# First norm of a decoder trunk in four quarters of the features, seven column tiles of the first FFN fed by each

## The chip, the core and the metric

The kernel runs on one core of one Trainium2 chip. The metric is device time in microseconds (us) of one execution. The core has five engines with a queue each, worked off in order: TensorE (PE, its weight loads PEld), VectorE (DVE), ScalarE (ACT), GpSimd (POOL) and SyncE (SP), which here only issues DMAs. Engines wait for each other and for DMAs by semaphores.

## The reference

Two layers act on a residual stream h of 512 tokens by 1024 features. Each sub-layer first normalises h, then scales and shifts it by numbers that come from a condition vector c:

```python
cond = jax.nn.silu(c)
for l in range(DEPTH):
    mod = cond @ ada_w[l] + ada_b[l]                      # 9 x 1024 numbers
    sh1, sc1, g1, sh2, sc2, g2, sh3, sc3, g3 = jnp.split(mod, N_MOD, axis=-1)
    hn = _modulate(_rms_norm(h, norm_g[l, 0]), sh1, sc1)  # xn * (1 + scale) + shift
    h = h + 0.5 * g1[:, None, :] * _swiglu(hn, ffn1_w_in[l], ffn1_w_out[l])
    hn = _modulate(_rms_norm(h, norm_g[l, 1]), sh2, sc2)
    z = hn @ w_in[l]
    ...                                                   # four token mixers, then w_out
    hn = _modulate(_rms_norm(h, norm_g[l, 2]), sh3, sc3)
    h = h + 0.5 * g3[:, None, :] * _swiglu(hn, ffn2_w_in[l], ffn2_w_out[l])

def _swiglu(x, w_in, w_out):
    gate, up = jnp.split(x @ w_in, 2, axis=-1)
    return (jax.nn.silu(gate) * up) @ w_out
```

The FFN is 2816 wide. What matters here is the very first norm: nothing of the first FFN can start before `sh1`, `sc1` (a product of c with 8 MB of weights) and the root mean square of x are there.

## The kernel before, in words

**Layout.** h is kept with features on the partitions: 8 tiles `h[k]` of 128 features x 512 tokens. Every product of the FFN is made three times, since each fp32 number is split into a high and a low fp32r part: `mm3` (L300 to 307) does high x high (L303), low activation x high weight (L304), high activation x low weight (L305). Weights come in chunks of [128, 2048]: a DMA on SP into a `raw` buffer (three of them), then `split_piece` rounds a part of it on ScalarE to `wh` (L271) and subtracts on VectorE to `wl` (L272). `proj_fm` opens four PSUM banks (pool `mm`) and runs them through the 8 feature tiles in two chunks of 4. A second PSUM pool, `at`, has four banks for everything small.

**The FFN.** `ffn` goes through the 22 hidden tiles in three parts (6, 8, 8). For each pair of hidden tiles one `proj_fm` makes two gate and two up tiles; the tile `i`. When a part's hidden tiles are done, the products with `w_out` follow; the tile `o`. Before the first `o` product stand 6 hidden tiles x 2 (gate, up) x 8 feature tiles x 3 = 288 products of 128x512.

**The start.** x comes in two DMAs (L386). ScalarE squares it (L598), TensorE transposes it into PSUM, ScalarE copies it to `h[k]` (L603). `rsqrt` (L177 on) takes the reciprocal root on VectorE, `bcast_tokens` spreads it over the partitions by TensorE (`bc_n`), and it stays in PSUM. `first_load` brings the weights of `sc1` (j = 1) and `sh1` (j = 0) by halves of the features (512 columns, rows of 2 KB). `partial_sums` adds up weight x cond over 8 tiles k: on VectorE (`accV`, L626 and 628) or as a product on ScalarE (L630, 633) that GpSimd adds (`accA`, L634); `SHARE` says which k goes where. `first_mod` sums over the partitions on TensorE (`adaps`), and VectorE adds the bias (`modc`, L646, 649). `scaled` makes `hn` on VectorE (L655), `shifted` rounds it to `hnh` on ScalarE (L659) and takes the rest `hnl` on VectorE (L660). `warm` is a run of products whose result nobody reads.

The first half of the features is done before the first FFN product; the second is done by `second_half`, which is issued between the first products. Later modulation weights come in steps of 1 MB (`ada_load`, `ada_step`: L454, 456), four to a group of 1024 numbers, with a reduction on VectorE (L465, 466) and one product by `fold` (also named `adaps`).

**What sets the order.** The code is recorded in a loop with a virtual clock for the helpers; then a scheduler orders the instructions of each engine and places buffers. `issue_after` only says what an instruction must stand behind on its own engine.

Of the kernel before, what the change touches and what calls it, by code (L numbers as in the profile page):

```python
# [24 lines left out]
def tile_hybrid_trunk(  # L25
# [49 lines left out]
    S1, S2, RS0, W0, W1 = 2.0, 3.0, 0, 20, 30  # L75
    SHARE = {(1, 0): "VVVVVVVV", (0, 0): "AAVVAAVV", (1, 1): "AAVVAVVV", (0, 1): "AVVVAVVV"}
# [184 lines left out]
    def split_piece(n, q):
# [50 lines left out]
    def proj_fm(name, nchunks, act, ks, evac, ranges=(FULL,), before=None):  # L312

        ps = [mmt(f"{name}_{m}") for m in range(4)]
        got = []
        for ri, (a, b) in enumerate(ranges):
# [3 lines left out]
            for ci in range(nchunks):  # L320
                if ci == 1 and not ahead[0]:
                    finish(startup)
                    ahead[0] = 2
# [4 lines left out]
                for m in range(4):  # L328
# [99 lines left out]
    def ada_load(n, tag="raw"):  # L428
# [76 lines left out]
    def first_load(j, e, tag):  # L505
        for q in range(2):
            r = wpool.tile([P, 2048], F32, tag=tag[q], name=f"fw{j}{e}{q}").rearrange("p (k d) -> p k d", k=4)
            src = ada_w[0, 4 * q * P : (4 * q + 4) * P, j * D + e * 512 : j * D + (e + 1) * 512]
            nc.sync.dma_start(out=r, in_=src.rearrange("(k p) d -> p k d", p=P))
            first_w[j, e, q] = r  # L510

    first_load(1, 0, ("raw", "raw"))
    first_load(0, 0, ("raw", "wl"))
    load_chunk(0)
    first_load(1, 1, ("wh", "wh"))
    first_load(0, 1, ("raw", "raw"))
# [97 lines left out]
    def partial_sums(j, e, q):  # L614


        for k in range(4 * q, 4 * q + 4):
            src = first_w[j, e, q][:, k % 4, :]
            how = SHARE[j, e][k]
            new = (j, e, how) not in begun  # L620
            if new:
                begun[j, e, how] = blk(name=f"acc{how}")
            acc = begun[j, e, how]
# [657 lines left out]
```

## Time and profile before

| | |
|---|---|
| median of 3 runs | 2001.35 us (2001.15 to 2002.89) |
| profiled execution | 1998.79 us |
| its span, first to last instruction | 1997.0 us |
| TensorE busy | 1960.0 us, 98% of the span |
| VectorE, ScalarE, GpSimd busy | 62%, 36%, 1% |
| DMA | 250.56 MB, mean 125 GB/s |
| mean granted clock of TensorE | 0.992 |

The table is of one execution, whose time stands 2.56 us below the median. A busy TensorE is not TensorE at its peak, since matmuls overlap: the pace is read from start to start. A granted clock of 1.00 is 2.4 GHz, 0.50 is 1.2 GHz.

### The profile page before, as it was taken

What the parts mean: (1) busy time and instruction counts of PE and PEld (TensorE: products, weight loads), DVE (VectorE), ACT (ScalarE), POOL (GpSimd) and SP (SyncE); (2) the same over time, 40 slices, a digit from 0 to 9 for tenths busy, and PEclk for the clock granted to TensorE, in tenths of its full rate; (3) what the DMA queues carried; (4) which work ended last, traced back from release to release, by engine and by line L of the source; (5) the groups of instructions that cost most, each with busy time, mean ns of one, the idle gap of its engine ahead of it and who ended that gap; (6) DMA issues with size and microseconds to landing.
All of it is one profiled execution on the core that took longest, in us unless ns stands there. A gap on an engine that the chain in (4) does not pass through costs nothing.

```text
span 1997.0 us, 26246 instructions
## 1 busy us (share of the span) xinstructions
PE 1960.0 (98%) x10339; PEld 1673.0 (84%) x10339; DVE 1230.1 (62%) x2595; ACT 726.4 (36%) x1513; POOL 24.3 (1%) x48
## 2 busy tenths in 40 slices
PE   7999999999999999999999999999999999999999
PEld 6788888897889888888898888889887898888888
DVE  7776765488877777676675433337898683333332
ACT  4323222344774423222342232333376543232230
POOL 2000000000000000000000000000000000000000
PEclk9999999999999999999999999999999999999999
DMA  8666655232211466566434323232212122423321
GB/s 286 215 203 208 214 189 186 85 91 64 69 43 47 154 201 231 184 217 211 148 106 147 118 93 106 85 106 91 64 64 70 43 64 85 127 86 104 106 64 43
DMA packets 157640, 250.56 MB, mean 125 GB/s; under 512 B 5748, under 2 KB 100428, under 8 KB 157516
## 3 DMA queue, kind: packets, MB, share of 16 engines
q1 hardware_dynamic: 156928, 247.73, 37.7%
q8 instruction: 81, 1.33, 0.3%
q0 software_dynamic: 352, 1.05, 0.2%
q14 instruction: 43, 0.35, 0.1%
q10 hardware_dynamic: 236, 0.10, 0.0%
HBM read 246.76 MB, written 2.10 MB: 125 GB/s over the span
## 4 chain that ended last, share of the span: by engine, by line
PE 93%; DVE 4%; ACT 1%; issue 1%; POOL 0%; DMA 0%; SPq 0%; ACTq 0%; POOLq 0%
PE i L304 16%; PE i L305 16%; PE i L303 16%; PE o L303 8%; PE o L304 8%; PE o L305 8%; PE wo L303 1%; PE wo L305 1%; PE wo L304 1%; PE scA L144 1%; PE scD L144 1%; PE poA L144 1%; DVE wl L272 1%; PE poD L144 1%; DVE cacc L953 1%
## 5 line engine op out<-in xcount | busy, mean ns | idle before, releaser
L272 DVE TENSOR_TENSOR wl<-w,wh 128x512 fp32r<-128x512 f32 (+2 forms) x664 | 410.6, 666 | 320.0 <-ACT wh L271 319.4
L271 ACT CAST wh<-w 128x512 fp32r<-128x512 f32 (+2 forms) x664 | 360.3, 602 | 655.8 <-issue 370.1
L304 PE MATMUL i<-hnl,wh 128*128 128x512 f32 (+1 forms) x1504 | 566.9, 378 | 4.0 <-DVE hnl L660 3.7
L303 PE MATMUL i<-hnh,wh 128*128 128x512 f32 (+1 forms) x1504 | 565.0, 378 | 4.1 <-ACT hnh L568 2.2
L305 PE MATMUL i<-hnh,wl 128*128 128x512 f32 (+1 forms) x1504 | 565.6, 377 | 0.0
L304 PEld LDWEIGHTS i<-hnl,wh 128*128 128x128 f32 x1504 | 284.2, 189 | 57.3 <-DVE hnl L660 6.0
L303 PEld LDWEIGHTS i<-hnh,wh 128*128 128x128 f32 x1504 | 283.2, 189 | 55.8 <-ACT hnh L568 2.6
L305 PEld LDWEIGHTS i<-hnh,wl 128*128 128x128 f32 x1504 | 284.3, 189 | 51.5
L303 PE MATMUL o<-acth,wh 128*128 128x512 f32 (+1 forms) x832 | 297.8, 358 | 0.0
L304 PE MATMUL o<-actl,wh 128*128 128x512 f32 (+1 forms) x832 | 296.7, 357 | 0.0
L305 PE MATMUL o<-acth,wl 128*128 128x512 f32 (+1 forms) x832 | 296.6, 356 | 0.0
L305 PEld LDWEIGHTS o<-acth,wl 128*128 128x128 f32 x832 | 157.2, 189 | 22.7
L303 PEld LDWEIGHTS o<-acth,wh 128*128 128x128 f32 x832 | 157.2, 189 | 22.4
L304 PEld LDWEIGHTS o<-actl,wh 128*128 128x128 f32 x832 | 157.2, 189 | 22.3
L456 DVE SCALAR_TENSOR_TENSOR acc<-ada,cond,acc 128x512 f32<-128x512 f32 x224 | 154.8, 747 | 32.1 <-DMA ada<-in_ada_w_dram 31.9
L776 DVE TENSOR_TENSOR silu<-silu,i 128x512 f32<-128x512 f32 x88 | 60.4, 687 | 170.5 <-PE i L305 170.5
L778 ACT CAST acth<-silu 128x512 fp32r<-128x512 f32 x88 | 54.4, 618 | 238.5 <-DVE silu L776 238.3
L708 DVE SCALAR_TENSOR_TENSOR h<-o,modc,h 128x512 f32<-128x512 f32 (+1 forms) x112 | 74.0, 671 | 70.8 <-PE o L305 70.2
L953 DVE SCALAR_TENSOR_TENSOR cacc<-yp,cwc,cacc 128x512 f32<-128x512 f32 x120 | 89.5, 746 | 1.6
L780 DVE TENSOR_TENSOR actl<-silu,acth 128x512 fp32r<-128x512 f32 x88 | 60.6, 689 | 28.2 <-ACT acth L778 28.2
L775 ACT ACTIVATE silu<-i 128x512 f32<-128x512 f32 x88 | 52.4, 595 | 37.1 <-PE i L305 37.1
L568 ACT ACTIVATE hnh<-hn,modc 128x256 fp32r<-128x256 f32 x80 | 38.8, 506 | 72.2 <-DVE hn L567 72.2
(298 smaller groups left out, 2228.4 us busy)
## 6 DMA issues: line engine op xcount, KB each, us to landing
w<-in_ffn_w_in_dram SPq DMA_DIRECT2D x176, 512.0 KB
ada<-in_ada_w_dram SPq DMA_DIRECT2D x64, 1024.0 KB
w<-in_ffn_w_out_dram SPq DMA_DIRECT2D x40, 1024.0 KB
w<-in_w_in_dram SPq DMA_DIRECT2D x18, 1024.0 KB
fw<-in_ada_w_dram SPq DMA_DIRECT2D x8, 1024.0 KB
w<-in_w_out_dram SPq DMA_DIRECT2D x8, 1024.0 KB
w<-in_ffn_w_out_dram SPq DMA_DIRECT2D x8, 512.0 KB
w<-in_w_in_dram SPq DMA_DIRECT2D x4, 520.0 KB
```

The costliest lines, as they stand in the source:

```text
L144: return T.matmul(out, **kw)
L271: A.copy(wh[:, a], r[:, a])
L272: V.tensor_tensor(wl[:, a], r[:, a], wh[:, a].bitcast(F32), ALU.subtract)
L303: T.matmul(ps, lhsT=lh, rhs=rh, start=start, stop=False)
L304: T.matmul(ps, lhsT=lh, rhs=rl, start=False, stop=False)
L305: last_t[0] = T.matmul(ps, lhsT=ll, rhs=rh, start=False, stop=stop)
L456: last_v[0] = V.scalar_tensor_tensor(acc, src, cond[:, k : k + 1], acc, ALU.mult, ALU.add)
L708: V.scalar_tensor_tensor(h[m][:, a:b], ps[:, a:b], mcol(l, j, m), h[m][:, a:b], ALU.mult, ALU.add)
L776: last_v[0] = V.tensor_tensor(s, s, ps[m], ALU.mult)
L778: A.copy(ah, s)
L780: V.tensor_tensor(al, s, ah.bitcast(F32), ALU.subtract)
L953: V.scalar_tensor_tensor(acc, ysl, w, acc, ALU.mult, ALU.add)
```

## The change

The features of the first norm are worked off in quarters (256 features, `Q`) where it was halves. Per quarter q: the weights of `sc1` and `sh1` come in rows of 1 KB; `partial_sums` takes both j, five k on VectorE and three on ScalarE with two adds on GpSimd; `first_mod` sums `accV` and `accA` in PSUM, so the adds that merged them go; two `h` tiles are scaled, shifted and rounded. The broadcast root is copied from PSUM to `rb0`, and two of the copies of h go to VectorE.

The first FFN part takes its 12 column tiles (6 gate, 6 up) in four groups (`FIRST`): 4 and 3 tiles that are open together in seven PSUM banks (four of `mm`, three of `at`) and get 2 x 7 x 3 = 42 products from each quarter, then 3 and 2 tiles as before. Splits of the first four chunks are two pieces instead of four. The parameter rows are loaded behind the last of these loads, and the later modulation steps start 28 instead of 20 us on the virtual clock.

```diff
     HX = 20
-    S1, S2, RS0, W0, W1 = 2.0, 3.0, 0, 20, 30
-    SHARE = {(1, 0): "VVVVVVVV", (0, 0): "AAVVAAVV", (1, 1): "AAVVAVVV", (0, 1): "AVVVAVVV"}
+
+    SHARE = {1: "VAVVAVAV", 0: "VAVVAVAV"}
+    Q = D // 4
+    W0, W1, M1, M2 = 20, 12, 2, 4
...
-    def ffn_chunks(wi, wo):
+
+    FIRST = (((0, 0, 2), (1, 0, 2)), ((0, 2, 4), (1, 2, 3)), ((1, 3, 4), (0, 4, 5), (1, 4, 5)), ((0, 5, 6), (1, 5, 6)))
+
+    def ffn_chunks(l, which, wi, wo):
...
+        def first_chunk(g, k0, nk):
+            src = [wi4[:, k0 : k0 + nk, i, a * P : b * P] for i, a, b in FIRST[g]]
+            add_chunk(src, nk, sum(x.shape[2] for x in src))
+
+        if l == 0 and which == 0:
+            for g, k0, nk in ((0, 0, 4), (1, 0, 4), (0, 4, 4), (1, 4, 4), (2, 0, 4), (2, 4, 4), (3, 0, 8)):
...
         r = wpool.tile([P, 2048], F32, tag=tag, name=f"ada{n}").rearrange("p (k d) -> p k d", k=2)
         src = ada_w[l, 2 * q * P : (2 * q + 2) * P, j * D : (j + 1) * D].rearrange("(k p) d -> p k d", p=P)
-        nc.sync.dma_start(out=r, in_=src)
+        with tc.issue_after(getattr(sp_last[0], "ins", sp_last[0])):
+            nc.sync.dma_start(out=r, in_=src)
         ada_raw[n] = r
...
+    def first_load(j, q):
+        src = ada_w[0, :, j * D + q * Q : j * D + (q + 1) * Q].rearrange("(k p) d -> p k d", p=P)
+        if (j, q) in ((1, 0), (0, 0), (1, 1)):
+            r = wpool.tile([P, 2048], F32, tag="wh", name=f"fw{j}{q}").rearrange("p (k d) -> p k d", k=KD)
+            nc.sync.dma_start(out=r, in_=src)
+            first_w[j, q] = [r[:, k, :] for k in range(KD)]
+            return
+        first_w[j, q] = []
+        for b in range(4):
+            r = blk(name="fwb").rearrange("p (k d) -> p k d", k=2)
+            nc.sync.dma_start(out=r, in_=src[:, 2 * b : 2 * b + 2, :])
+            first_w[j, q] += [r[:, 0, :], r[:, 1, :]]
+
+    def first_loads(q):
+        first_load(1, q)
+        first_load(0, q)
+        for g in range(2):
+            d = load_rows(2 * (q // 2) + g, 2 * (q % 2), 2 * (q % 2) + 2)
+        return d
+
+    first_loads(0)
+    first_loads(1)
+    sp_last = [None]
+
...
+    def turned(k):
         ps = mmt(f"xt{k}")
         for t in range(NT):
             transpose(out=ps[:, t * P : (t + 1) * P], in_=xraw[t // 2][:, t % 2, k * P : (k + 1) * P], identity=ident)
-        A.copy(h[k], ps)
+        if k < 2:
+            V.tensor_copy(h[k], ps)
+        else:
+            A.copy(h[k], ps)
+
+    turned(0)
+    turned(1)
     load_columns()
-    r = rsqrt(ss0, NT, 1.0 / D, "n000", RS0)
-    rb0 = bcast_tokens(r, NT, "n000")
+    r = rsqrt(ss0, NT, 1.0 / D, "n000")
+    rbp = bcast_tokens(r, NT, "n000")
+    rb0 = blk(name="rb0")
+    V.tensor_copy(rb0, rbp)
...
+    def first_mod(j, q, behind=None):
+
+        acc = begun[j, q]
+        ps = att(f"adaps0{j}{q}")
+        es = ExitStack()
+        if behind is not None:
+            es.enter_context(tc.issue_after(getattr(behind, "ins", behind)))
+        with es:
+            for m in range(2):
+                for how in "VA":
+                    last_t[0] = matmul(ps[:, m : m + 1], lhsT=acc[how][:, m * P : (m + 1) * P], rhs=ones[:, 0:1],
+                                       start=how == "V", stop=how == "A")
+        mod = modc[:, j, 2 * q : 2 * q + 2]
+        V.tensor_tensor(mod, ps[:, :2], adab[:, 0, j * KD + 2 * q : j * KD + 2 * q + 2], ALU.add)
...
+    def open_banks():
+        first_ps[0] = [mmt(f"ia{m}") for m in range(4)]
+        first_ps[1] = [att(f"ib{m}") for m in range(3)]
+
+    def first_products(q):
+
+        marks = []
+        for g in range(2):
+            n = 2 * (q // 2) + g
+            wh, wl = first_parts[n]
+            for m, ps in enumerate(first_ps[g]):
+                ws = slice(m * P, (m + 1) * P)
+                for k in (2 * q, 2 * q + 1):
+                    kk = k % 4
+                    mm3(ps, wh[:, kk, ws], wl[:, kk, ws], act0[k][0], act0[k][1], k == 0, k == KD - 1)
+                marks.append(last_t[0])
+        return marks
+
+    first_parts = {}
+
+    def split_rows(q):
+        for g in range(2):
+            n = 2 * (q // 2) + g
+            split_piece(n, q % 2, 2)
+            nk = chunks[n][1]
+            first_parts[n] = (splits[n] if n in splits else
+                              tuple(w.rearrange("p (k c) -> p k c", k=nk) for w in parts[n]))
 
     warm(W0)
-    partial_sums(1, 0, 0)
...
+    def startup():
+        open_banks()
+        marks = first_products(0)
+        for q in range(4):
+            if q < 3:
+                partial_sums(1, q + 1)
+                partial_sums(0, q + 1)
+                split_rows(q + 1)
+                if q < 2:
+                    sp_last[0] = first_loads(q + 2)
+                else:
+                    load_chunk(4)
+                first_mod(1, q + 1, marks[M1])
+                scaled(q + 1)
+                first_mod(0, q + 1, marks[M2])
+                shifted(q + 1)
+                marks = first_products(q + 1)
...
+            if l == 0 and i == 0 and hf == 0:
+                tiles = [[(w, j) for w, a, b in g for j in range(a, b)] for g in FIRST]
+                startup()
+                with tc.issue_after(getattr(sp_last[0], "ins", sp_last[0])):
+                    load_params()
+                ahead[0] = 2
+                for g in range(2):
+                    for m, ps in enumerate(first_ps[g]):
+                        gated(*tiles[g][m], ps)
+                for n in range(4):
+                    splits.pop(n)
+                for g, nchunks in ((2, 2), (3, 1)):
+                    proj_fm(f"i{l}{i}f{g}", nchunks, hn, list(range(KD)),
+                            lambda m, ps, ri, rng: gated(*tiles[g][m], ps[m]), nm=len(tiles[g]))
...
-    startup = start(second_half())
     hn, before = act0, None
     for l in range(L):
-        gen = start(ada_gen(36 * l + 36 if l == 0 else 36 * (l + 1)), delay=20.0 if l == 0 else AD)
+        gen = start(ada_gen(36 * l + 36 if l == 0 else 36 * (l + 1)), delay=28.0 if l == 0 else AD)
         hn2 = {}
         before = ffn(l, 0, hn, before, (l, 1, hn2))
```

**ScalarE, the start.** `sq0` are the squares of x, `h..` the copies of the transposed tiles, `accA` the first modulation sum. Before:

```order
L598 ACTIVATE sq0_168,ss0_165<-x0_124 128x1024
L598 ACTIVATE sq0_170,ss0_165<-x1_126 128x1024 [waits DMAHW4_49]
L598 ACTIVATE sq0_172,ss0_165<-x1_126 128x1024
L603 COPY h0_157<-xt0_174 128x512 [waits PE_49]
L603 COPY h1_158<-xt1_180 128x512 [waits PE_49]
L603 COPY h2_159<-xt2_186 128x512 [waits PE_49]
```

Now:

```order
L638 COPY h5_167<-xt5_312 128x512 [waits PE_49]
L638 COPY h6_168<-xt6_318 128x512 [waits PE_49]
L638 COPY h7_169<-xt7_324 128x512 [waits PE_49]
L629 ACTIVATE sq0_171,ss0_170<-x0_124 128x1024 [waits DMAHW1_49]
L629 ACTIVATE sq0_173,ss0_170<-x0_124 128x1024
L629 ACTIVATE sq0_175,ss0_170<-x1_126 128x1024 [waits DMAHW4_49]
L629 ACTIVATE sq0_177,ss0_170<-x1_126 128x1024
L668 ACTIVATE accA_256<-fw10_138,cond_132 128x256 [waits DMAHW5_49,DVE_49]
```

The four squares, from which the root is taken, stood ahead of the copies of h and now stand behind the six that ScalarE still makes.

**TensorE, from one quarter to the next.** `ia`, `ib` are the seven open tiles, `adaps011` and `adaps001` the scale and the shift of the second quarter. Before, where the second half's scale `adaps011` stood:

```order
L303 MATMUL i000_2_440<-hnh_380,wh0_370 128x512
L304 MATMUL i000_2_440<-hnl_381,wh0_370 128x512
L144 MATMUL adaps011_457<-ones_99,accV_367 128x1 [waits DVE_49,PE_49]
L144 MATMUL adaps011_457<-ones_99,accV_367 128x1 x3
L305 MATMUL i000_2_440<-hnh_380,wl0_371 128x512
L303 MATMUL i000_2_440<-hnh_386,wh0_370 128x512
L304 MATMUL i000_2_440<-hnl_387,wh0_370 128x512
```

Now, the last products of the first quarter and the first of the second:

```order
L324 MATMUL ib2_371<-hnl_348,wh1_340 128x512
L325 MATMUL ib2_371<-hnh_347,wl1_341 128x512
L146 MATMUL adaps011_468<-ones_99,accV_414 128x1 [waits DVE_49,PE_49]
L146 MATMUL adaps011_468<-ones_99,accA_415 128x1 [waits Pool_49]
L146 MATMUL adaps011_468<-ones_99,accV_414 128x1
L146 MATMUL adaps011_468<-ones_99,accA_415 128x1
L146 MATMUL adaps001_479<-ones_99,accV_428 128x1 [waits DVE_49]
L146 MATMUL adaps001_479<-ones_99,accA_429 128x1 [waits Pool_49]
L146 MATMUL adaps001_479<-ones_99,accV_428 128x1
L146 MATMUL adaps001_479<-ones_99,accA_429 128x1
L323 MATMUL ia0_365<-hnh_485,wh0_336 128x512 [waits Activation_49]
L324 MATMUL ia0_365<-hnl_486,wh0_336 128x512 [waits DVE_49]
```

What were single summing products among those of the first half now stands behind all 42 of a quarter, scale and shift one after the other, with nothing between them and the next quarter.

**VectorE, the second modulation group after the first norm.** `ada15` is its last step, `ared16` what `adaps04` on TensorE waits for, `wl10`, `wl11`, `wl12` low parts of chunks. Before:

```order
L272 TENSOR_TENSOR wl10_1081<-w10_1039,wh10_1080 128x512 [waits DMAHW4_49,DMAHW3_49,Activation_49]
L272 TENSOR_TENSOR wl10_1081<-w10_1039,wh10_1080 128x512 [waits Activation_49] x3
L456 SCALAR_TENSOR_TENSOR acc120_903<-ada15_1114,cond_132,acc120_903 128x512 [waits DMAHW0_49,DVE_49]
L456 SCALAR_TENSOR_TENSOR acc121_904<-ada15_1114,cond_132,acc121_904 128x512 [waits DVE_49]
L456 SCALAR_TENSOR_TENSOR acc120_903<-ada15_1114,cond_132,acc120_903 128x512 [waits DVE_49]
L456 SCALAR_TENSOR_TENSOR acc121_904<-ada15_1114,cond_132,acc121_904 128x512 [waits DVE_49]
L465 STREAM_TRANSPOSE acct0_1121<-acc120_903 128x512 [waits DVE_49]
L465 STREAM_TRANSPOSE acct1_1124<-acc121_904 128x512 [waits DVE_49]
L466 TENSOR_REDUCE ared16_1120<-acct0_1121 128x16 [waits DVE_49]
L466 TENSOR_REDUCE ared16_1120<-acct1_1124 128x16 [waits DVE_49]
L272 TENSOR_TENSOR wl11_1155<-w11_1090,wh11_1154 128x512 [waits DMAHW6_49,DMAHW7_49,PE_49,Activation_49]
```

Now:

```order
L292 TENSOR_TENSOR wl12_1247<-w12_1189,wh12_1246 128x512 [waits DMAHW0_49,DMAHW1_49,PE_49,Activation_49]
L292 TENSOR_TENSOR wl12_1247<-w12_1189,wh12_1246 128x512 [waits Activation_49] x3
L474 SCALAR_TENSOR_TENSOR acc120_1047<-ada15_1262,cond_132,acc120_1047 128x512 [waits DMAHW5_49,DVE_49]
L474 SCALAR_TENSOR_TENSOR acc121_1048<-ada15_1262,cond_132,acc121_1048 128x512 [waits DVE_49]
L474 SCALAR_TENSOR_TENSOR acc120_1047<-ada15_1262,cond_132,acc120_1047 128x512 [waits DVE_49]
L474 SCALAR_TENSOR_TENSOR acc121_1048<-ada15_1262,cond_132,acc121_1048 128x512 [waits DVE_49]
L483 STREAM_TRANSPOSE acct0_1269<-acc120_1047 128x512 [waits DVE_49]
L483 STREAM_TRANSPOSE acct1_1272<-acc121_1048 128x512 [waits DVE_49]
L484 TENSOR_REDUCE ared16_1268<-acct0_1269 128x16 [waits DVE_49]
L484 TENSOR_REDUCE ared16_1268<-acct1_1272 128x16 [waits DVE_49]
```

The step has moved from in front of a chunk that is split late to behind one. On TensorE `adaps04` stood before between the products of a tile of `o` in the middle of a chunk; now it stands behind the last product of chunk 10 and ahead of the first of chunk 11, and chunk 12 follows 9 in its `wh` buffer.

## Rows read from the trace of the kernel before

**Rows 1.** The profile's page, part 1: busy time, share of the span, instructions, by engine.

```profile
PE 1960.0 (98%) x10339; PEld 1673.0 (84%) x10339; DVE 1230.1 (62%) x2595; ACT 726.4 (36%) x1513; POOL 24.3 (1%) x48
```

**Rows 2.** Timeline, TensorE: start, duration, line, operation, tile, shape, [idle before, releaser].

```profile
32.92 1.19 PE L303 MATMUL i<-hnh,wh 128*128 128x512 f32 x4 [1.01 <-ACT hnh L659]
...
69.88 0.39 PE L303 MATMUL i<-hnh,wh 128*128 128x512 f32 x1
...
90.28 0.39 PE L303 MATMUL i<-hnh,wh 128*128 128x512 f32 x1
...
109.36 0.48 PE L303 MATMUL o<-acth,wh 128*128 128x512 f32 x1
```

**Rows 3.** Timeline, TensorE around the second half of the first norm.

```profile
48.28 0.95 PE L144 MATMUL adaps<-ones,accV 128*128 128x1 f32 x8
...
50.89 0.96 PE L303 MATMUL i<-hnh,wh 128*128 128x512 f32 x3 [0.84 <-ACT hnh L659]
53.37 0.80 PE L304 MATMUL i<-hnl,wh 128*128 128x512 f32 x1 [1.52 <-DVE hnl L660]
53.97 0.63 PE L305 MATMUL i<-hnh,wl 128*128 128x512 f32 x1
...
55.67 0.63 PE L303 MATMUL i<-hnh,wh 128*128 128x512 f32 x1
```

**Rows 4.** Stages of 2 us: length, busy (instructions) by engine, PEclk, DMA share, GB/s.

```profile
14.00:16.00 2.00, 2.00 (x19) 1.95 (x20) 1.96 (x10) 1.05 (x3) 0.00 (x0) 1.00 1.04 384
...
20.00:22.00 2.00, 0.36 (x4) 0.36 (x4) 2.00 (x4) 1.33 (x2) 1.00 (x1) 1.00 1.03 348
22.00:24.00 2.00, 2.00 (x12) 2.00 (x12) 1.97 (x3) 0.00 (x0) 1.92 (x2) 0.56 1.06 383
...
50.00:52.00 2.00, 1.00 (x4) 0.48 (x3) 2.00 (x5) 1.89 (x3) 0.00 (x0) 1.00 1.02 337
...
54.00:56.00 2.00, 2.00 (x6) 1.25 (x5) 2.00 (x4) 0.88 (x2) 0.00 (x0) 0.50 0.00 0
```

**Rows 5.** Timeline, ScalarE: the squares of x, the copies of h, one chunk's rounding.

```profile
8.99 1.06 ACT L598 ACTIVATE sq<-x 128x1024 bf16<-128x1024 f32 x1 [1.04 <-DMA x<-in_x_dram]
...
11.09 3.97 ACT L603 COPY h<-xt 128x512 f32<-128x512 f32 x8
...
52.72 2.16 ACT L271 CAST wh<-w 128x512 fp32r<-128x512 f32 x4
```

**Rows 6.** Timeline, VectorE: the first instruction behind the reciprocal root.

```profile
14.23 0.47 DVE L626 TENSOR_SCALAR accV<-fw,cond 128x512 f32<-128x512 f32 x1
```

**Rows 7.** Timeline, TensorE: transposes of x, broadcast of the root, two warm-up runs.

```profile
9.01 4.94 PE L148 MATMUL xt<-ident,x 128*128 128x128 f32 x30 [2.54 <-DMA x<-in_x_dram]
...
14.26 1.10 PE L144 MATMUL bc_n<-ident,ry_n 128*128 128x128 f32 x8
...
22.83 8.29 PE L144 MATMUL warm<-ident 128*128 128x128 f32 x60
```

**Rows 8.** Groups by line and shape, VectorE: count, busy us, mean ns.

```profile
L567 DVE SCALAR_TENSOR_TENSOR hn<-h,modc,bc_n 128x256 f32<-128x256 f32 x80 | 36.4, 475 | 7.0 <-PE bc_n L144 7.0
```

**Rows 9.** Timeline, GpSimd and VectorE: a sum beside a GpSimd add, and alone.

```profile
28.09 1.27 POOL L634 TENSOR_TENSOR accA<-accA,prod 128x512 f32<-128x512 f32 x1 [3.71 <-ACT prod L633]
...
28.29 1.62 DVE L638 TENSOR_TENSOR accV<-accV,accA 128x512 f32<-128x512 f32 x1
...
46.69 0.69 DVE L638 TENSOR_TENSOR accV<-accV,accA 128x512 f32<-128x512 f32 x1
```

**Rows 10.** Timeline, VectorE: a later modulation step, its reduction, one chunk's low halves.

```profile
130.87 2.74 DVE L456 SCALAR_TENSOR_TENSOR acc<-ada,cond,acc 128x512 f32<-128x512 f32 x4 [0.91 <-DMA ada<-in_ada_w_dram]
133.52 1.30 DVE L465 STREAM_TRANSPOSE acct<-acc 128x512 f32<-128x512 f32 x2
134.74 1.24 DVE L466 TENSOR_REDUCE ared<-acct 128x16 f32<-128x512 f32 x2
137.33 2.50 DVE L272 TENSOR_TENSOR wl<-w,wh 128x512 fp32r<-128x512 f32 x4 [1.34 <-ACT wh L271]
```

More of the change, by code (lines that the diff above doesn't have):

```diff
@@ L327, in proj_fm @@
                 nk = wh.shape[1]
-                for m in range(4):
+                for m in range(nm):
                     for kk in range(nk):
@@ L503, in tile_hybrid_trunk @@
     first_w = {}
[L505 to L516, printed above, removed]
+    def first_load(j, q):
[15 more added lines that the diff above has]
+            d = load_rows(2 * (q // 2) + g, 2 * (q % 2), 2 * (q % 2) + 2)
+        return d
+    first_loads(0)
+    first_loads(1)
+    sp_last = [None]
     h = [hpool.tile([P, S], F32, name=f"h{k}") for k in range(KD)]
@@ L612, in warm, with partial_sums @@
             matmul(ps[:, :P], lhsT=ident, rhs=ident, start=True, stop=True)
[L614 to L623, printed above, removed]
+    def partial_sums(j, q):
+        acc = {how: blk(name=f"acc{how}")[:, :Q] for how in "VA"}
+        new = {"V": True, "A": True}
+        for k in range(KD):
+            how = SHARE[j][k]
+            src, a, ck = first_w[j, q][k], acc[how], cond[:, k : k + 1]
@@ L652, in scaled @@
-    def scaled(e):
-        for k in range(4 * e, 4 * e + 4):
-            begun[k, "t"] = blk(name="hn0")
-            last_v[0] = V.scalar_tensor_tensor(begun[k, "t"], h[k], mcol(0, 1, k), rb0, ALU.mult, ALU.mult)
-    def shifted(k):
-        hh, hl = act0[k] = (blk(F32R, "hnh"), blk(F32R, "hnl"))
-        A.activation(hh, begun[k, "t"], AF.Identity, bias=mcol(0, 0, k))
-        V.scalar_tensor_tensor(hl, begun[k, "t"], mcol(0, 0, k), hh.bitcast(F32), ALU.add, ALU.subtract)
+                if new[how]:
+                    V.tensor_scalar(a, src, ck, None, ALU.mult)
+                else:
+                    last_v[0] = V.scalar_tensor_tensor(a, src, ck, a, ALU.mult, ALU.add)
+            elif new[how]:
+                A.activation(a, src, AF.Copy, scale=ck)
+            else:
+                prod = blk(name="prod")[:, :Q]
+                A.activation(prod, src, AF.Copy, scale=ck)
+                G.tensor_tensor(a, a, prod, ALU.add)
@@ new lines, in scaled, with shifted @@
+    def scaled(q):
+        for k in (2 * q, 2 * q + 1):
+            begun[k, "t"] = blk(name="hn0")
+            last_v[0] = V.scalar_tensor_tensor(begun[k, "t"], h[k], modc[:, 1, k : k + 1], rb0, ALU.mult, ALU.mult)
+    def shifted(q):
+        for k in (2 * q, 2 * q + 1):
+            hh, hl = act0[k] = (blk(F32R, "hnh"), blk(F32R, "hnl"))
+            A.activation(hh, begun[k, "t"], AF.Identity, bias=modc[:, 0, k : k + 1])
+        for k in (2 * q, 2 * q + 1):
+            hh, hl = act0[k]
+            V.scalar_tensor_tensor(hl, begun[k, "t"], modc[:, 0, k : k + 1], hh.bitcast(F32), ALU.add, ALU.subtract)
@@ L768, in ffn @@
         for hf, (lo, hi) in enumerate(PARTS):
[L769 to L785 removed]
+            act, gates = {}, {}
@@ new lines, in ffn, with evac @@
+            if l == 0 and i == 0 and hf == 0:
[12 more added lines that the diff above has]
+                            lambda m, ps, ri, rng: gated(*tiles[g][m], ps[m]), nm=len(tiles[g]))
+            else:
+                for j in range(lo, hi, 2):
+                    def evac(m, ps, ri, rng, j=j):
+                        if rng[1] == S and m >= 2:
+                            gated(0, j + m - 2, ps[m - 2])
+                            gated(1, j + m - 2, ps[m])
+                    early = j == 0 and before is not None
+                    proj_fm(f"i{l}{i}{j}", 2, hn, list(range(KD)), evac,
+                            HALVES if early else (FULL,), before if early else None)
```

132 lines of the change are left out of this document (48 added, 84 removed).

## The prediction

> **What bounds the kernel now.** I read the page's busy shares first: TensorE works 98% of the span [rows 1], so time is gained or lost only where TensorE stands or runs slowly. Then the timeline of TensorE. Once it runs, products start 0.2267 us apart (90 of them from 69.88 to 90.28) [rows 2]; no change of the start can alter that. The change ends where the first product with `w_out` (`o`) starts, 109.36, and both kernels make the same 288 products before it: 288 x 0.2267 = 65.3 us. The kernel before therefore carries 109.36 - 65.3 = 44.1 us of start: 32.9 until the first product [rows 2], and 11.1 of standing and slow running behind it. The worst of that is at the second half: from the summing products at 48.28 it takes 2.6 us to the next product that needs their result (50.89), another 2.5 until its low part is there (53.37), and then products start 0.425 us apart (four from 53.97 to 55.67) [rows 3], at a granted clock of 0.50, 1.2 GHz [rows 4]. So the question is whether four quarters carry less than 44.1 us. All sums are against the profiled execution (1998.79); the median of the runs is 2.56 above it.
>
> **1. The first product comes no earlier.** A quarter needs half the weights, but ScalarE's order decides. x is there at 8.99 as before [rows 5]: SP's first two loads are unchanged. Transposes run 0.165 us apart (4.94 for 30) [rows 7]; the first of those that ScalarE copies is ready after 13 of them, 11.2, and six copies of 0.50 (3.97 for 8) [rows 5] end at 14.2, or at 15.0 if the transposes set their pace; I take 14.5. Only then come the four squares, 2.1 for two (8.99 to 11.09) [rows 5]: 18.7, where they ended at 11.1. The root takes 3.1 (11.09 to 14.23) [rows 5, 6], its broadcast 1.1 [rows 7]: 22.9. The copy to `rb0` is in no row: from 0.3 to the 0.69 of a VectorE sum (2.74 for four) [rows 10]; I take 0.6, nearer to the latter since it reads PSUM. The modulation sums stand behind it on VectorE and start at 23.5, against 14.23 [rows 6]: 9.3 us later, whenever their weights landed.
>
> From there: ten sums of 256 columns. One takes 475 ns [rows 8]; those of 512 start 0.66 apart (130.87 to 133.52 for four) [rows 10], 256 columns fewer take 0.27 off: 0.40 each, 4.0, so 27.5. Their buffers then serve the first weight chunk: 1,024 columns rounded on ScalarE and subtracted on VectorE, 1.2 each by 2.50 for 2,048 [rows 10]: 29.9. TensorE has meanwhile 20 warm-up products, 40 records; 60 took 8.29 with a clock of 0.56 in the first stage [rows 4, 7], so 5.5: 28.4; two rounds of summing products of 0.95 [rows 3]: 30.3. Then modulation, a piece of 768 columns that VectorE has in front (0.9), `hn`, `hnh`: 50.89 - 49.23 = 1.7 [rows 3] and 0.9. The first product starts at 32.9 to 35 (where the clock is low for the broadcast too); I take 33.4: **+0.5 us**. Removed with the halves: three merging adds on VectorE, 0.69 each [rows 9], which lay beside TensorE's waits; nothing for them.
>
> **2. Three waits between quarters.** By the order shown, scale and shift of the next quarter are summed behind all 42 products, whatever the code's marks allow. Seven open tiles leave one free bank in the small pool, so the shift's sums also wait until VectorE has read the scale's. The 2.6 us of the second half (48.28 to 50.89) [rows 3] grow by a second 0.95, by about 0.25 for that reading and by 0.3 until the first low part is there (two `hn` of 0.66 in front of it, then itself): 4.1 each, **12.3**. The next products stand behind them on TensorE, and nothing is there to fill in.
>
> Each wait is followed by slow products: 3 us at 0.425 instead of 0.2267 lose 1.4 [rows 3, 4]; three times, **4.2**. The rows alone show both: after the short wait at 50.89 the stage still reads 1.00, after the longer one 0.50 [rows 4]. The Trainium skill (TensorE: Matmul & The Clock Gate, section "HAM oscillation — how this bites in real kernels") says that a wait between short groups of matmuls sends the clock down and lets each group start slow, every time, and advises longer runs between waits. By that rule this term is 4.2, and without it the sum ends 4.9 lower, which is the first rival.
>
> Does the rest of a quarter fit under the 42 products (9.5 plus the slow 1.4)? On VectorE: the last `hnl` 1.3, sums 4.0, splits of about 1,800 columns 2.2, and what GpSimd's four adds cost it. A sum beside an add of 512 took 1.62, alone 0.69 [rows 9]: 0.93. An add of 256 is in no row; 0.47 by its size, 0 to 0.93 as bounds: 1.9 a quarter (0 to 3.7). Together 9.4 of 10.9: hidden, 0.3 late at the upper bound. In front of the last quarter's sums VectorE also has eight instructions of a later modulation step, 5 us, while most of its splits are done: about **1.0** late. ScalarE and GpSimd have less than that. The first quarter's products meet late low parts, **0.8**; one reduction product and three transposes in front of `o` take **0.7**. Sum 12.3 + 4.2 + 1.0 + 0.8 + 0.7 = 19.0 against 11.1: **+7.9 us**.
>
> **3. A new wait behind the first norm.** `adaps04` on TensorE waits for `ared16`, whose VectorE chain now stands behind chunk 12, which cannot be rounded before chunk 9's last product has freed its buffer. From there: first rounding 0.65, `wl12` 2.4, four sums 2.65, two transposes 1.2, two reductions 1.24 [rows 10]: 8.2. TensorE has only chunk 10's 24 products, 5.4. It stands **2.8**; a low clock behind it costs 0 to 1.4, I take **0.8**: **+3.6 us**. Everything later is back to back, and gives nothing back.
>
> Sum: 0.5 + 7.9 + 3.6 = +12.0, an execution of 2010.8; on the median, 2001.35 + 12.0 = **2013.4; I predict 2013**. Its own range: first product -1 to +1.5, GpSimd -0 to +1, clock -2 to +0.6, the wait of part 3 -1 to +1: 2009 to 2017.
>
> **Rivals.** *The clock holds.* The waits contain summing products, and TensorE is never still for more than some 2.5 us. Then 4.2 and 0.8 go: +7.0, 2008. For it the stage at 50 us, against it those at 22 and 54 [rows 4].
>
> *The quarters overlap (faster).* The marks in the code put scale and shift behind the third and fifth tile of a quarter; were they issued there, they would be through while two to four tiles are left. The point that decides is whether a quarter's wait stays under 1.2 us: at none, 12.3, 4.2 and the 1.0 go, leaving +12.0 - 17.5 = -5.5, 1996. Against it stands the order, in which the wait is written down.
>
> *The early start counts.* If the first product comes as much earlier as the squares came late (7.6 us) and the clock holds, +12.0 - 7.6 - 5.0 = -0.6: no change, 2001. Against it: VectorE's sums stand behind the root in its queue.
>
> *The loads bind.* On SP the fourth chunk waits for a raw buffer, which VectorE frees with the first chunk's second split, near 34 us; behind it stand a 1 MB step of the later modulation, the third quarter's 2 MB and the next chunk. These 0.8 + 1.05 + 2.1 MB need 11.3 us at 348 GB/s, the rate in a stage with rows of 1 KB (384 in one with 2 KB) [rows 4]: 45, against sums that start near 50 (33.4, the first 42 products with their 0.8, a wait of 4.1, and `hnl`). If the smaller rows (some now 512 B) halve the rate, they land at 57, and the third quarter is some 6 late: 2019. The Trainium skill (DMA: Bandwidth & Descriptors, section "Specifications") puts line rate at transfers of 512 B and more; by it the rate is 384 and this rival is out. The stage of 20 us, below that rate with rows of 1 KB, does not agree, so it stays in.
>
> **How the numbers follow.** Forecast 0.62, clock holds 0.20, loads bind 0.06, overlap 0.06, early start 0.06. The range 2004 to 2019 takes in the first three and leaves out some 0.14 below and 0.04 above. About 0.2% (4 us) can be told from no change: faster 0.06 (overlap); same 0.10 (early start, and a tail of the clock's rival); slower 0.84.
>
> **What would show it.** In the profile after: squares on ScalarE from 14 us on, first modulation sum near 23.5, first product near 33; three gaps of about 4 us on TensorE between groups of 42, each followed by a stage near 0.50; `o` from 117 to 119; a wait of nearly 3 us at the product by `fold` some 35 us later. If `o` starts before 109, part 1 or 2 is wrong: squares early, or the summing products between the tiles. If the time is over 2019, the loads were late: VectorE's sums would then wait for `fwb` DMAs.

## The result, and the profile after

The changed kernel takes 2015.5 us (median; 2015.2 to 2017.4), against 2001.3 (2000.8 to 2002.9) for the kernel before: a ratio of 1.0072, 95% interval 1.0054 to 1.0089. The prediction was 2013, range 2004 to 2019. The mechanism is the one predicted; three of its terms were too small, so that its working is 7.4 us short, and something later in the program gave part of that back.

TensorE is still busy 98% of the span, as in [rows 1]. Timeline of TensorE after the change, the rows that answer to [rows 2, 3, 7]:

```profile
24.80 2.08 PE L146 MATMUL bc_n<-ident,ry_n 128*128 128x128 f32 x8 [10.01 <-DVE ry_n L191]
26.67 6.33 PE L146 MATMUL warm<-ident 128*128 128x128 f32 x40
...
37.28 1.19 PE L323 MATMUL ia<-hnh,wh 128*128 128x512 f32 x4
...
47.54 0.28 PE L146 MATMUL adaps<-ones,accV 128*128 128x1 f32 x2
...
51.73 0.80 PE L323 MATMUL ia<-hnh,wh 128*128 128x512 f32 x1 [1.67 <-ACT hnh L702]
...
64.27 0.28 PE L146 MATMUL adaps<-ones,accV 128*128 128x1 f32 x2
...
68.39 2.07 PE L323 MATMUL ia<-hnh,wh 128*128 128x512 f32 x4 [1.87 <-ACT hnh L702]
...
80.92 0.28 PE L146 MATMUL adaps<-ones,accV 128*128 128x1 f32 x2
...
84.84 2.08 PE L323 MATMUL ia<-hnh,wh 128*128 128x512 f32 x4 [1.68 <-ACT hnh L702]
...
96.07 0.39 PE L323 MATMUL i00f<-hnh,wh 128*128 128x512 f32 x1
...
123.86 0.47 PE L323 MATMUL o<-acth,wh 128*128 128x512 f32 x1
...
156.40 0.39 PE L325 MATMUL o<-acth,wl 128*128 128x512 f32 x1
159.39 0.41 PE L146 MATMUL adaps<-ared,fold 128*128 128x32 f32 x2 [2.61 <-DVE ared L484]
160.14 0.77 PE L323 MATMUL i<-hnh,wh 128*128 128x512 f32 x1 [0.34 <-DVE h L781]
...
163.54 0.40 PE L325 MATMUL i<-hnh,wl 128*128 128x512 f32 x1
```

A record is one line of the trace; the summing and warm-up products show as two records each. Read the timeline from landmark to landmark. The first product comes at 37.28 instead of 32.92: +4.4. `o` comes at 123.86 instead of 109.36: +14.5. Between the two stand 65.3 us of products and 21.3 us of standing and slow running (11.1 before): three waits of 4.2, 4.1 and 3.9 (from the first sum `adaps` to the next product), 12.2 in all; groups of 42 products that take 12.5, 12.5 and 11.2 behind a wait where 9.5 would do, 7.7 in all; 0.7 in the first group, 0.6 in front of `o`. Then the new wait for `ared`.

Stages of 2 us of the same kernel, columns as in [rows 4]: the clock behind the first wait falls to 0.50 and is back at 58 us; one stage behind the second and one behind the third wait follow.

```profile
48.00:50.00 2.00, 1.47 (x13) 1.36 (x12) 1.12 (x3) 0.00 (x0) 0.00 (x0) 1.00 1.09 357
50.00:52.00 2.00, 0.34 (x2) 0.27 (x1) 1.77 (x4) 1.04 (x2) 0.00 (x0) 0.68 1.10 348
52.00:54.00 2.00, 2.00 (x5) 1.21 (x6) 1.97 (x4) 2.00 (x6) 0.77 (x1) 0.50 1.17 314
54.00:56.00 2.00, 2.00 (x6) 1.61 (x5) 2.00 (x4) 0.74 (x2) 1.86 (x3) 0.50 1.17 300
56.00:58.00 2.00, 2.00 (x7) 1.52 (x7) 2.00 (x5) 0.00 (x0) 0.47 (x1) 0.62 1.01 323
58.00:60.00 2.00, 2.00 (x11) 1.64 (x10) 0.81 (x2) 0.00 (x0) 0.00 (x0) 1.00 0.97 305
...
68.00:70.00 2.00, 1.61 (x4) 1.32 (x5) 2.00 (x5) 2.00 (x5) 0.17 (x1) 0.50 0.13 37
...
86.00:88.00 2.00, 2.00 (x7) 1.52 (x5) 0.30 (x1) 0.00 (x0) 0.00 (x0) 0.50 1.06 339
```

Timeline of VectorE in the root, the copy and the first sum; ScalarE's squares and GpSimd's adds follow in fences of their own. They answer to [rows 5, 6].

```profile
19.75 0.17 DVE L182 TENSOR_SCALAR rv_n<-ss 128x4 f32<-128x4 f32 x1 [8.19 <-ACT sq L629]
...
20.36 1.10 DVE L189 SCALAR_TENSOR_TENSOR rt_n<-ry_n,rv_n 128x1 f32<-128x1 f32 x4
21.38 1.43 DVE L191 SCALAR_TENSOR_TENSOR ry_n<-rt_n,ry_n 128x1 f32<-128x1 f32 x4
...
24.60 0.35 DVE L191 SCALAR_TENSOR_TENSOR ry_n<-rt_n,ry_n 128x1 f32<-128x1 f32 x4
26.91 0.69 DVE L646 COPY rb<-bc_n 128x512 f32<-128x512 f32 x1 [1.96 <-PE bc_n L146]
27.52 0.34 DVE L664 TENSOR_SCALAR accV<-fw,cond 128x256 f32<-128x256 f32 x1
```

```profile
15.43 1.09 ACT L629 ACTIVATE sq<-x 128x1024 bf16<-128x1024 f32 x1
...
19.50 0.21 ACT L629 ACTIVATION_READ_ACCUMULATOR sq<-x 128x1 f32 x1
```

```profile
20.59 3.02 POOL L672 TENSOR_TENSOR accA<-accA,prod 128x256 f32<-128x256 f32 x4 [18.14 <-ACT prod L671]
```

The squares end at 19.7, 1.0 later than the forecast's 18.7. The root takes 5.2 us (19.75 to 24.95), not the 3.1 of [rows 5, 6]: its first two steps of four instructions take 1.10 and 1.43 while GpSimd adds, the last one 0.35 when it has ended. Single instructions show how: four of them, one for each add, last 0.69 to 0.75 and end some 0.02 after an add does; the others last 0.14 to 0.22, as they do without adds. The broadcast takes 2.08, twice the 1.10 of [rows 7], at a granted clock of 0.50 (24 to 26 us); TensorE had stood for 10 us.

By the first broadcast of a later norm the profiled executions are 19.4 us apart (399.3 and 418.7), at the end only 16.4. The kernel before lost the difference by itself. Stages of 4 us of the kernel before, then the place in the changed kernel that answers to the first:

```profile
664.00:668.00 4.00, 4.00 (x22) 4.00 (x23) 4.00 (x11) 2.54 (x5) 0.00 (x0) 0.58 0.02 4
1504.00:1508.00 4.00, 2.99 (x20) 2.72 (x21) 3.77 (x13) 3.26 (x12) 0.00 (x0) 0.88 0.57 145
1508.00:1512.00 4.00, 4.00 (x22) 3.54 (x21) 2.26 (x8) 1.08 (x4) 0.00 (x0) 0.69 0.47 184
```

```profile
684.00:688.00 4.00, 4.00 (x36) 4.00 (x35) 4.00 (x12) 2.04 (x4) 0.00 (x0) 1.00 0.02 4
```

At these clocks 1.7 us are lost in the first stretch (4 x 0.42) and 1.7 in the other two (4 x 0.12 + 4 x 0.31). The waits in front of them, 1.1 and 2.3 us, stand in both kernels alike; only the clock behind them differs, and of the ten profiles of this document four show a low clock behind the first of these waits and three behind the second. So I take them for chance; no kernel was profiled twice to test that. The profiled execution of before was, besides, 2.5 us below the median, that after 0.4: hence 14.3 between the medians.

### The profile page after: what moved, and what is told of

Same layout as the page of the kernel before. It is cut to its first block, busy times and chain, and to the rows that moved or that the text cites. A ratio compares the mean times of both kernels' runs of the same rounds, so it can differ in the third digit from the quotient of the medians.

```text
span 2013.4 us, 26343 instructions
## 1 busy us (share of the span) xinstructions
PE 1964.5 (98%) x10335; PEld 1676.3 (83%) x10335; DVE 1233.3 (61%) x2614; ACT 729.5 (36%) x1522; POOL 28.7 (1%) x58
## 5 line engine op out<-in xcount | busy, mean ns | idle before, releaser
L292 DVE TENSOR_TENSOR wl<-w,wh 128x512 fp32r<-128x512 f32 (+4 forms) x660 | 410.7, 669 | 335.1 <-ACT wh L291 334.4
L291 ACT CAST wh<-w 128x512 fp32r<-128x512 f32 (+4 forms) x660 | 360.4, 605 | 671.2 <-issue 382.1
L323 PE MATMUL i<-hnh,wh 128*128 128x512 f32 (+1 forms) x1408 | 527.3, 376 | 2.6 <-ACT hnh L599 2.2
L324 PE MATMUL i<-hnl,wh 128*128 128x512 f32 (+1 forms) x1408 | 527.7, 375 | 0.3
L325 PE MATMUL i<-hnh,wl 128*128 128x512 f32 (+1 forms) x1408 | 526.9, 375 | 0.0
L323 PEld LDWEIGHTS i<-hnh,wh 128*128 128x128 f32 x1408 | 264.5, 189 | 50.1 <-ACT hnh L599 2.6
L324 PEld LDWEIGHTS i<-hnl,wh 128*128 128x128 f32 x1408 | 265.3, 189 | 48.1 <-DVE hnl L592 0.7
L325 PEld LDWEIGHTS i<-hnh,wl 128*128 128x128 f32 x1408 | 265.1, 188 | 47.8
```

The source lines that it names most:

```text
L291: A.copy(wh[:, a], r[:, a])
L292: V.tensor_tensor(wl[:, a], r[:, a], wh[:, a].bitcast(F32), ALU.subtract)
L323: T.matmul(ps, lhsT=lh, rhs=rh, start=start, stop=False)
L324: T.matmul(ps, lhsT=lh, rhs=rl, start=False, stop=False)
L325: last_t[0] = T.matmul(ps, lhsT=ll, rhs=rh, start=False, stop=stop)
```

## The experiments

All are edits of the changed kernel. Each was timed beside the kernel before (2000.7 to 2001.2 in these runs). In the cuts of code `issue_after(x)` stands for `issue_after(getattr(x, "ins", x))`; `...` and the notes behind `#` are added here.

**Squares first.**

```diff
+        last_sq = A.activation(sq, ..., AF.Square, ...)
 ...
+            with tc.issue_after(last_sq):
+                A.copy(h[k], ps)
```

> On ScalarE the four squares stand ahead of the six copies of h (one issue_after); nothing else is edited. Theory A (ScalarE's order sets the start): the squares end near 13.3 us instead of 19.7, the root ends before GpSimd's adds begin, so it takes 3.1 instead of 5.0, the broadcast and everything behind it come 8 to 9 us earlier, first product near 28.5, the three waits stay 4 us each: 2006 to 2008. Rival B (the loads bind): the sums at the start or those of the third quarter then wait for their weights, and 3 us or less of the 9 arrive at the end: 2012 to 2015. Rival C (the start is a minor part, as the prediction had it with +0.5): 2014 to 2016.

Measured: 2003.9 (2002.1 to 2006.0), ratio to before 1.0016 (1.0007 to 1.0024): 11.7 less than the changed kernel. Root on VectorE, then the first product on TensorE:

```profile
11.79 0.16 DVE L182 TENSOR_SCALAR rv_n<-ss 128x4 f32<-128x4 f32 x1
...
12.39 0.61 DVE L189 SCALAR_TENSOR_TENSOR rt_n<-ry_n,rv_n 128x1 f32<-128x1 f32 x4
```

```profile
28.25 1.22 PE L323 MATMUL ia<-hnh,wh 128*128 128x512 f32 x4
```

The root starts at 11.8 and takes 3.1 again, the first product comes at 28.25, 9.0 earlier: theory A, though the time lies 2 us below its range. The other 2.7 lie between the first product and `o`, 112.04: 18.5 us beside the products, not 21.3, with the waits nearly as before (4.1, 3.9, 3.9). Of this, 1.9 are slow running behind the waits, 5.8 where it was 7.7. The same three waits brought 7.1 in the run with the delay of 20 below, so this part may be chance; the 9.0 are what the order is worth. Only a little of B shows: the rounding in front of the first `hnh` waits 2.2 us for its weights.

**No GpSimd adds.**

```diff
-                prod = blk(name="prod")[:, :Q]
-                A.activation(prod, src, AF.Copy, scale=ck)
-                G.tensor_tensor(a, a, prod, ALU.add)
+                acc[f"A{k}"] = blk(name="prod")[:, :Q]
+                A.activation(acc[f"A{k}"], src, AF.Copy, scale=ck)
 ...
-                for how in "VA":
+                for i, how in enumerate(acc):
```

> ScalarE's three products of each sum are kept apart and TensorE adds them up with VectorE's sum (16 summing products a quarter instead of 8), so GpSimd's 4 adds a quarter go. Theory A (the root was slow because GpSimd added beside it): the root falls from 5.0 to 3.1 or 3.4 us, the broadcast comes 1.6 to 1.9 us earlier; the extra summing products cost some 0.9 us in each of three waits, so the time moves by -1.9 + 2.7 = +1 at most and -1 at least: 2014 to 2016.5. Rival B (another cause): the root still takes 5.0 us and the time rises by about 3: 2018.

Measured: 2020.0 (2018.1 to 2020.3). The time lies beyond both theories, but the root decides between them:

```profile
20.32 0.61 DVE L189 SCALAR_TENSOR_TENSOR rt_n<-ry_n,rv_n 128x1 f32<-128x1 f32 x4
20.85 0.36 DVE L191 SCALAR_TENSOR_TENSOR ry_n<-rt_n,ry_n 128x1 f32<-128x1 f32 x4
```

With the squares as late as ever and no adds beside it the root takes 3.1 (19.71 to 22.81): GpSimd's adds cost it 2.1. My price for the remedy was wrong. Sixteen summing products take 3.5 us where eight took 1.7, and each wait grows by more than 2 (6.4, 7.2 and 6.2, 19.9 in all); the 24 warm-up records in front of the first product then take 4.5 us instead of 2.9, so it still comes at 37.8. `o` comes 6.5 later; at `fold` nothing waits in this order.

**Waits filled with warm-up products.**

```diff
+            if behind is not None:
+                for _ in range(2 if j == 1 else 6):
+                    last_t[0] = matmul(ps[:, P : 2 * P], lhsT=ident, rhs=ident, start=True, stop=True)
         mod = modc[:, j, 2 * q : 2 * q + 2]
```

> Warm-up products (two behind the scale's sums, six behind the shift's) stand in each of the three waits between quarters, in the bank of the sums. Theory A (the slow clock behind a wait comes from TensorE standing still): the 42 products behind each wait run at 0.2267 us from the start, the waits stay 4.1 us: 7 us are saved, 2008 to 2009. Rival B (the narrow summing products and the short stands are enough for the low clock): nothing changes, 2015 to 2017.

Measured: 2011.0 (2010.3 to 2016.4), between the two theories. Behind the first filled wait the clock is low all the same, behind the second it is not:

```profile
52.00:54.00 2.00, 0.66 (x4) 0.36 (x2) 1.30 (x3) 0.45 (x1) 0.00 (x0) 0.50 1.19 306
54.00:56.00 2.00, 1.68 (x4) 1.39 (x5) 1.85 (x4) 2.00 (x5) 0.19 (x1) 0.50 1.16 298
...
70.00:72.00 2.00, 1.31 (x6) 1.09 (x7) 1.68 (x3) 2.00 (x5) 0.00 (x0) 1.00 0.34 66
```

The slow running falls from 7.7 to 1.9 us, but the waits grow from 12.2 to 17.9, because VectorE reads the sums only when the products behind them in the same bank are through. `o` starts at 123.71, nothing gained; the 4.6 us come from the wait at `fold`, which the new order does not have. So the longer waits hide what the clock is worth; the next run keeps the two apart.

**Five warm-up products in a bank of their own.**

```diff
                 first_mod(0, q + 1, marks[M2])
+                with tc.issue_after(last_t[0]):
+                    warm(5)
```

> The changed kernel with five warm-up products in each wait between quarters, in a bank of their own behind the shift's sums, so that VectorE's reading of the sums does not wait for them (in the filled run it did: the waits grew from 12.2 to 17.9 us). The product by fold stands some 9 rows further back on TensorE, so its wait of 2.6 us and what is behind it (4.9 in all) go too, as in the runs before. Theory A (the slow products behind a wait come from what TensorE does in the last microseconds of the wait): the waits stay at 4.0 to 4.4, the 42 products of a quarter take 9.5 to 10 us instead of 12.5, the first product with w_out starts near 117 to 118, not 123.9: 2004 to 2006. Rival B (five of them are too few, or the clock is low for the summing products already): 12.5 us for the 42 products again, w_out near 124, 2010 to 2012.

Measured: 2009.0 (2007.6 to 2011.1), between the two theories; `o` at 122.05, and no wait at `fold`. The waits are 4.3, 4.5 and 5.1. The first two groups of 42 take 10.9 and 9.7 us instead of 12.5 each; the clock was low behind the first and the third wait:

```profile
52.00:54.00 2.00, 2.00 (x9) 1.81 (x9) 1.87 (x3) 2.00 (x4) 0.00 (x0) 0.51 1.13 333
...
68.00:70.00 2.00, 2.00 (x12) 1.55 (x11) 2.00 (x4) 2.00 (x6) 0.78 (x1) 1.00 0.05 20
...
84.00:86.00 2.00, 2.00 (x6) 1.61 (x5) 0.42 (x1) 0.00 (x0) 0.00 (x0) 0.50 1.09 339
```

The slow running is 3.2 in all. Unfilled waits of 4 us brought 1.5 to 3.2 each (7.7, 7.1 and 5.8 for the three, in the profiles of the changed kernel, of the delay of 20 and of the squares first). Behind the second wait only 0.1 us are left in both filled runs, so there the filling keeps the clock. The 1.4 to 1.7 behind the first wait of both, and behind the third of this run, are hardly less than an unfilled wait can bring, so there nothing is shown. Why these differ from the second stays open.

**Sums between the tiles.** The products go in three calls a quarter, each behind what was issued last on TensorE:

```diff
+            mark = first_products(q, 0, M1)          # M1, M2 = 5, 6
             ...
+                first_mod(1, q + 1, mark)
                 scaled(q + 1)
+            mark = first_products(q, M1, M2)
+                first_mod(0, q + 1, mark)
                 shifted(q + 1)
+            first_products(q, M2, 7)
```

> The products of the last two tiles of a quarter are made to stand behind the next quarter's sums on TensorE: the scale's sums behind the fifth tile, the shift's behind the sixth. Theory A (the waits are only a matter of order: sums behind all 42 products): three waits of 4.1 us shrink to about 1 each and the clock stays up, so 12.2 + 7.7 less some 3 go: 1997 to 2001, against 2015.5 and 2001.3 for the two kernels. Rival B (VectorE is not through with the next quarter's sums by then): TensorE stands at the sums themselves, and 5 us or less are saved: 2010 to 2014.

Measured: 2001.9 (2000.6 to 2002.4), ratio to before 1.0006 (0.9997 to 1.0015): 13.6 less than the changed kernel, no different from the kernel before. TensorE around the second and third quarter:

```profile
50.41 1.20 PE L323 MATMUL ia<-hnh,wh 128*128 128x512 f32 x4 [0.33 <-ACT hnh L702]
...
57.36 0.28 PE L146 MATMUL adaps<-ones,accV 128*128 128x1 f32 x2
...
59.65 0.28 PE L146 MATMUL adaps<-ones,accV 128*128 128x1 f32 x2
...
63.48 0.74 PE L323 MATMUL ia<-hnh,wh 128*128 128x512 f32 x2 [1.41 <-ACT hnh L702]
...
112.23 0.48 PE L323 MATMUL o<-acth,wh 128*128 128x512 f32 x1
```

Between groups TensorE now stands 0.3 and 1.4 us, in the last case not at all, and no group runs slowly: `o` is 11.6 earlier with the first product where it was (37.10). Theory A, 0.9 above its range; VectorE has its sums ready. No wait remains at `fold` either, so the 13.6 are not the quarters' waits alone: 11.6 of them stand at `o`.

**Later modulation steps at 20 instead of 28.**

```diff
-        gen = start(ada_gen(...), delay=28.0 if l == 0 else AD)
+        gen = start(ada_gen(...), delay=20.0 if l == 0 else AD)
```

> The later modulation steps start 20 instead of 28 us on the virtual clock, as in the kernel before; everything else is the changed kernel. Theory A (part 3 of the prediction: the product by fold waits for a reduction that stands behind chunk 12 on VectorE, and only its place in the order makes it wait): the wait of 2.6 us, the 0.3 us behind it and the 7 slow products after it (1.4 us) go, the start stays as it is: 2010.5 to 2012. Rival B (the reduction is late wherever it stands, since the start came late): a wait of 2 us or more shows at another product by fold, and the time is 2014 to 2016. Rival C (the steps come back between the quarters' sums on VectorE and lengthen the three waits): 2016 to 2019.

Measured: 2012.8 (2012.2 to 2013.8), 2.7 less. The start is unchanged (`o` at 123.83), and nothing waits at `fold`:

```profile
123.83 0.47 PE L323 MATMUL o<-acth,wh 128*128 128x512 f32 x1
153.88 0.30 PE L146 MATMUL adaps<-ared,fold 128*128 128x32 f32 x2
```

By the next norm's broadcast this execution is 4.9 us ahead of the changed kernel's (413.8 and 418.7), at the end 2.6: theory A by its mechanism, 0.8 above its range, with 2.3 lost again later.

**Both.** Squares first, sums between the tiles, and for chunks 4 to 6:

```diff
+        if 4 <= n < 7:
+            es.enter_context(tc.issue_after(low[2]))      # the third quarter's last hnl
+        with es:
             V.tensor_tensor(wl[:, a], r[:, a], wh[:, a].bitcast(F32), ALU.subtract)
```

> Squares ahead of the copies, the quarter's sums behind the fifth and the sixth tile, and the low parts of the next chunk behind the third quarter's low parts on VectorE. Theory A (the two losses are separate: a late start, some 9 us with 2.5 of slow clock, and the waits between quarters, some 13.6): both go, first product near 28.2, the first product with w_out near 104 to 106 against 109.4 in the kernel before, 1993 to 1997. Rival B (with the earlier start the quarters' sums or their weights are late, so that what the start gains is lost at the sums): the waits between quarters come back with 2 us or more each, 1998 to 2002, no better than one of the two edits alone.

Measured: 1993.0 (1990.9 to 1994.7), ratio to before 0.9958 (0.9944 to 0.9971): 0.4% faster than the kernel before, 1.1% than the changed one.

```profile
27.91 1.20 PE L327 MATMUL ia<-hnh,wh 128*128 128x512 f32 x4 [0.21 <-ACT hnh L707]
...
41.56 1.20 PE L327 MATMUL ia<-hnh,wh 128*128 128x512 f32 x4 [1.36 <-ACT hnh L707]
...
55.47 0.50 PE L327 MATMUL ia<-hnh,wh 128*128 128x512 f32 x1 [2.24 <-ACT hnh L707]
...
106.31 0.47 PE L327 MATMUL o<-acth,wh 128*128 128x512 f32 x1
```

Theory A: `o` at 106.3, 3.1 before the kernel before. Something of B is there too: the waits that the other run had at 0.3 and 1.4 are 1.4 and 2.2 here. Of the 7.7 us to the kernel before only these 3.1 are shown to come from the start: the profiled executions are 4.6 apart, and the rest lies later in the program, where no run looks for it. The third edit was not run alone.

**The scale's sums behind the fourth tile.** As before, with `M1, M2 = 4, 6`.

> As the run before (squares first, sums between the tiles), but the scale's sums stand behind the fourth tile instead of the fifth, the shift's behind the sixth as there. Theory A (VectorE needs the time between the two sums for hn, and the rest of the wait is the hnh behind the second sums): the wait behind the third quarter shrinks by up to 1 us, but TensorE stands up to 1 us at the scale's sums: the time is within 2 us of the run before. Rival B (VectorE's sums are the limit): the stand at the scale's sums is 1.4 us or more in each quarter, 2 to 4 us slower than the run before.

Measured: 1995.2 (1993.6 to 1998.3), ratio to before 0.9972 (0.9960 to 0.9983), 2.2 slower than the run above, at the edge of both theories and with overlapping intervals. TensorE stands 1.8, 0.6 and 0.7 us at the scale's sums, which VectorE therefore has late at this place in every quarter, clearly so in the first. In front of the second quarter's products the wait shrinks from 1.36 to 0.17, in front of the third's it is 2.23 as in the run above: that one does not hang on where the scale's sums stand.

## Why the prediction was right, and where it was short

**Part 1, "the first product comes no earlier", +0.5: right in sign, measured +4.4.** The chain is the one named (copies, squares, root, sums in that order), and the sums take the 4.0 given (27.52 to 31.54). The first product comes 3.9 behind the 33.4 forecast, where at most 1.5 was allowed for. Too small were: the six copies and four squares, by 1.0; the root, by 2.1, where I carried over 3.1 although the order puts ScalarE's products and with them GpSimd's adds beside it (the price of an add beside a VectorE sum stood in [rows 9] and was used only for the sums); the broadcast and the 40 warm-up records behind it, by 1.4, at a granted clock of 0.50 from 24 to 30 us after TensorE had stood for 10. What follows took 0.6 less than forecast. The warm-up records end at 32.83, 1.3 after VectorE's sums, so at its end the chain runs through them and not through the sums. That this chain carries the start is shown by the first experiment, that the adds slow the root by the second. The Trainium skill (SBUF — State Buffer, section "SBUF: two separate sides") says that a VectorE operation with two SBUF inputs and a GpSimd operation that reads SBUF exclude each other for the whole instruction; the trace agrees: four such instructions, of one element a partition, last until an add of 0.72 to 0.73 us ends.

**Part 2, +7.9, measured +10.1.** The three waits were sized well: 12.3 forecast, 12.2 measured; so were the low parts (0.8 and 0.74) and the step in front of `o` (0.7 and 0.58). The mis-sized term is the clock: 7.7, not 4.2, and 5.8 to 7.7 in the three profiles with the same waits. Behind the first wait the low clock starts before the wait ends (0.68 from 50 to 52) and lasts some 5.7 us of products, 12 of them at 0.425 us or more, where 3 us were carried over from [rows 3, 4], behind a shorter wait. The 1.0 for late sums of the last quarter was not there: the eight modulation instructions fit. The rule that the prediction took from the Trainium skill (TensorE: Matmul & The Clock Gate, section "HAM oscillation — how this bites in real kernels"), that each group behind a wait starts slow, holds for the three groups here (0.50 at 52, 68 and 86 us). The prediction's "4.9 lower" without it is 5.0 by its own terms (4.2 and 0.8), as its first rival has it. Putting the sums between the tiles removes waits and slow running together.

**Part 3, +3.6, measured +4.9.** TensorE stands 2.8 us as forecast (156.6 to 159.4); the products behind it lose 1.6 by the clock (8 from 160.14 to 163.54, at 0.2267 they are 1.8) and 0.5 in front of the first, for the 0.8 given. That it is a matter of place only, the run with the delay of 20 shows.

**The sum.** 4.4 + 10.1 + 4.9 = 19.4 against 12.0. "Everything later is back to back, and gives nothing back" failed: 3.0 us that the kernel before lost to a low clock were not lost after. So the number is nearer to the measurement than its working: 12.0 forecast, 16.4 between the profiled executions, 14.3 between the medians. That is luck: with the 19.4 the forecast of the median would have been near 2021, outside the range. It is inside because the kernel before lost 3.0 us later on and because its profiled execution, from which the sum starts, stood 2.5 below its median and that of the changed kernel only 0.4.

**The rivals.** *The clock holds* fell at the three stages of 0.50. *The quarters overlap* did not happen in this order, but the run with the sums between the tiles made it happen and gained 11.4 us between the first product and `o` (and the wait at `fold`), where the rival had 17.5: the mechanism was right. Its point of decision, waits under 1.2 us, held for two of the three (0.3, 1.4 and none). *The early start* became real with the squares in front: the first product comes 9 us earlier, where 7.6 were named. *The loads bind* fell: no sum waits for a weight DMA at 1 KB rows (348 to 357 GB/s from 48 to 52 us).

## What to carry to other kernels

Cutting a stage into finer steps multiplies its hand-over: price one hand-over (standing, plus the slow products behind it) and multiply, before counting what the finer step starts earlier. Then look in the order, not in the code, for what stands between: here two orders that the scheduler chose (copies ahead of squares, sums behind all 42 products) cost 9.0 us at the first product and 11.4 behind it, and with both set, and one more edit, the kernel with quarters is 0.4% faster than the one with halves. And check a forecast by its parts: here two of them (the first product, the clock) lay outside their ranges while the total lay inside. When instructions move, look for which other engine now works beside them.

## What the runs showed of the hardware

GpSimd's adds of 128x256 slow even VectorE instructions of 128x1: four of them took 1.10 and 1.43 us beside adds, 0.61 and 0.36 without, since one instruction for each add lasts until the add is through. Warm-up products do not reliably keep the clock: of five or eight in each wait the second wait's kept it at 1.00 in both runs and the first wait's did not (0.50 and 0.51 from 52 to 54 us). A wait of 1.1 us that stands in all ten profiles was followed by a low clock in four of them. The summing products, one column wide, come 0.11 us apart at the high clock (16 records in 1.7 us), each of them twice, so doubling their number cost more here (4.5 us in the whole kernel) than the GpSimd adds that it saved.
